# A second seven-product group in the output projection of the last layer

## The chip, the core and the metric

The kernel runs on one core of a Trainium2 chip. Its time is the device time of one execution in microseconds, as the median of several runs; less is better. Before the change it takes 1976.4 us (median of 3 runs, 1975.78 to 1977.06). Engines are named as the profile names them: PE (TensorE, matmuls), PEld (its weight loads), DVE (VectorE), ACT (ScalarE), POOL (GpSimd, which here only issues DMAs), SP (SyncE, which issues most DMAs).

## What is computed

Two layers of a decoder trunk over 256 tokens of width 2048, in float32. Each layer normalises its input, makes one wide projection, runs three token mixers on it (A: sparse attention, B: a convolution module, C: stick-breaking attention), projects each mixer's output to the model width, merges the three with sigmoid gates, and adds an output projection to the residual:

```python
y_a = (dsa_attention(qa, ka, va, qi, ki, wi, top_k) * jax.nn.silu(za)) @ w_a_out
y_b = (conformer_conv(ub, conv_w, conv_b, cln_w, cln_b) * jax.nn.silu(zb)) @ w_b_out
y_c = (stick_breaking_attention(qc, kc, vc) * jax.nn.silu(zc)) @ w_c_out
g = jax.nn.sigmoid(gates).reshape(b, s, N_BRANCH, D_MODEL)
merged = g[:, :, 0] * y_a + g[:, :, 1] * y_b + g[:, :, 2] * y_c
return x + merged @ w_out
```

After the second layer a last RMSNorm closes the trunk. The change touches `merged @ w_out` of the second layer: 256 tokens x 2048 (K) times 2048 x 2048.

## The kernel before

**Split numbers.** Each float32 operand is split in a high part (a cast, on ACT) and a low part (the rest, on DVE), and a product is three matmuls: high x high, low x high, high x low. Weights come from DRAM in units of 256 rows (K) x 512 columns, 512 KB, into a `raw` buffer (five, and `va` as a sixth). `high` casts a unit into `wh` (L296), `low` writes `raw - wh` into `wl` (L300). There are three pairs of `wh` and `wl`, so a unit's pair comes free when PE has done the unit three places before it; both run two steps ahead of PE.

**Steps.** `run` goes through a list of steps that is written out by hand with `gather`. A *plain* unit is twelve matmuls (3 products x 2 token tiles x 2 rows of 128). A *half step* is six and belongs to a `Seven`.

**Seven products.** `Seven` does a block product of 2 token tiles x 2 halves of a K range x 2 column blocks with seven block products instead of eight (M1 to M7, each in halves a and b). Four of them (M5, M6, M7, M4) take sums of weight blocks, and three (M5 to M7, M3) sums of token blocks. The weight sums are made in *homes*: buffers into which two blocks are loaded (`two`, `three`), added on DVE (L555, L570, or L557, L558 in another form) and on the way in by accumulating DMAs that POOL issues (L545, L576). A number `adds` chooses the form: 3 uses three DVE sums per half and one accumulating DMA, 4 uses two and two. The results build up in four PSUM banks X, Y, Z, W; banks are copied (L621, ACT) and subtracted (L627, DVE) on the way. A step's `at` hangs work on it, such as these sums.

**The stage.** The last layer ends so: a group `h1` for gates of branch B, with the first eight units of B's output product (`y1`) among its steps; the other eight y units (columns 1024 to 1535, then 1536 to 2047); and the output projection. Each four y units complete one of four column blocks j of the merged activations. That block is multiplied and added (L1612, L1613), transposed on DVE (L340), sent through DRAM in DMAs from POOL (`z`, L343, and back as `zy`, L349), and split again by ACT and DVE (L713, L714) into `mx`, the left operand of the output projection. The number LATER says how many steps after its product a block is split. `output_sums` makes the token sums from blocks j = 0 and 1.

**The output projection before.** One group `o` does columns 0 to 1023 for the first half of K (rows 0 to 1023). Everything else is plain units: c (columns 1024 to 1535, eight units), d (1536 to 2047, first half of K, four units), e and f (0 to 511 and 512 to 1023, second half of K, four units each). Units of the second half of K need j = 2 (their first two) and j = 3. Each finished column block is added to the residual (`emit_x`, L1646 or L1649). Columns 1536 to 2047, second half, come last: their four weight units are loaded and split (L285, into `s`), and 54 matmuls follow behind the last step, then the norm and the output.

`o`'s homes before are the buffers `ar`, `ph` and `pl`, which the groups before it also use. `slot()` gives one of 13 buffers of 8 KB a partition (`s8`).

Of the kernel before, what the change touches and what calls it, by code (L numbers as in the profile page):

```python
# [89 lines left out]
def trunk(ctx: ExitStack, tc: tile.TileContext, x, w_in, xt, w_a, w_b, w_c, w_out,  # L90
# [54 lines left out]
    def slot(dt=F32):  # L145
        return sp.tile([P, KC, S], dt, tag="s8", bufs=13, name=nm("s8"))
# [668 lines left out]
    for layer in range(DEPTH):  # L815
# [775 lines left out]
        def mg(j, t, mgs=mgs):  # L1591
            return mgs[j // 2][:, j % 2, t, :]
# [85 lines left out]
        def merged(b, j, y):  # L1678
            sg = held.pop((b, j), None)
            with in_turn() if b == 1 else nullcontext():  # L1680
                merge(b, j, y, sg)
            if b == 1:
                with in_turn():
                    turned([mg(j, t) for t in range(NT)], partial(use_m, j), LATER - 3 * (j in (1, 3) and not last), soon=True)

        kept_x, acc3 = {}, once(wide_accs)

        def output(q, banks, k0):
            if last and q == 3:
# [66 lines left out]

        zg["M4", 1].at(1, partial(gate_summed, 0))
        zg["M3", 1].at(1, partial(gate_summed, 1))
        for i, st in enumerate((y1[2][3], f1[0]) if not last else y1[3][:2]):
            st.at(0, partial(output_sums, i * 2, i * 2 + 1))  # L1760
        if last:
            zd[3].at(0, lambda: nc.sync.dma_start(fwl[0], fnw.partition_broadcast(P)))
        if last:
            o = Seven(wo, (p0 * 512, p0 * 512 + 512), mx, osums, 10, None, 3)
            qs = {}
            for q in range(4):
                own = q in (p0, p0 + 1)
                banks = (lambda v: lambda: [o.bank(n) for n in v])("ZW" if q - p0 else "XY") if own else None
                qs[q] = output(q, banks, KC if own else 0)
# [21 lines left out]
        steps += gather(thin + rest, y=y2[10:], g=g1, c=c1, d=d1)  # L1791
        if last:
            steps += gather("y*2 " + begin.replace("M6a y", "M6a").replace("M2a y", "M2a") + rest, g=h1, y=y1[:8], c=e1, d=f1)
            steps += y1[8:]
        else:
            steps += gather("y*2 " + begin.replace("M6a y", "M6a").replace("M2a y", "M2a") +
                            "g.M3a c g.M3b c g.M4a c g.M4b c y*4", g=h1, y=y1[:12], c=e1)
# [10 lines left out]
        steps[at_norm].at(0, norm)  # L1808
        c, d = 2 - p0, 3 - p0
        if last:  # L1810
            steps += qs[c][:4] + gather(
                "g.M1a d g.M5a g.M1b d g.M5b d g.M6a d g.M6b c g.M2a c g.M2b g.M7a g.M7b g.M3a e g.M3b e g.M4a f g.M4b f c*2 e*2 f*2",
                g=o, c=qs[c][4:], d=qs[d], e=qs[p0], f=qs[p0 + 1])
        else:
            second = ("n.M1a h n.M1b h*3 y n.M5a y n.M5b y n.M6a n.M6b y n.M2a n.M2b n.M7a n.M7b "
                       "o.M1a c o.M1b d o.M5a c o.M5b d o.M6a n.M4a o.M6b n.M4b c*2 o.M2a d o.M2b o.M7a o.M7b n.M3a n.M3b d "
                       "o.M3a e o.M3b e o.M4a e o.M4b e f*4")
            steps += gather(second, n=n, o=o, y=y1[12:], h=f1, c=qs[c], d=qs[d], e=qs[p0], f=qs[p0 + 1])
# [15 lines left out]
            nc.vector.tensor_scalar(half, known, -0.5 / D, -0.5 * EPS, op0=ALU.mult, op1=ALU.add)  # L1834
            nc.vector.tensor_scalar(known, known, 1.0 / D, EPS, op0=ALU.mult, op1=ALU.add)

        c0, n = 1536, 512
        xc = residual(c0, n)

        head = acc3()  # L1840
        accs = [head[0], acc_tile()]
        nc.vector.tensor_add(xc[:, 1, :], head[1], xc[:, 1, :])
        oh, ol = ([slot(F32R).rearrange("p (k a) t -> p k (a t)", a=2) for _ in range(2)] for _ in range(2))
        for k0 in range(0, KC, 2):
            ks = slice(k0 % 4, k0 % 4 + 2)
            unit(w_out[layer], KC + k0, 2, [(c0, n)], dst=(oh[k0 // 4][:, ks, :], ol[k0 // 4][:, ks, :]))
        for t in range(NT):
            m, r, b = (small(1) for _ in range(3))
            kn, hf, ss = known[:, t:t + 1], half[:, t:t + 1], ssq[:, t, 3:4]
            if t < NT - 1:  # L1850
                for h in range(2):
                    token_products([accs[t]], n, (oh[h], ol[h]), mx, KC + h * 4, 4, KD, [t])
                emit_x(xc, [accs[t]], 3, c0, [t])
            else:

                token_products([accs[t]], n, (oh[0], ol[0]), mx, KC, 4, KD, [t], KC)
                token_products([accs[t]], n, (oh[1], ol[1]), mx, KC + 4, 2, KD - 2, [t], KC)
# [85 lines left out]
```

## Time and profile before

| | us |
|---|---|
| median of 3 runs | 1976.4 |
| the profiled execution | 1976.76 |
| its span, first to last instruction | 1974.7 |
| PE busy | 1962.6 |
| DVE busy | 1724.7 |
| ACT busy | 1357.5 |
| POOL busy | 234.2 |
| first y unit behind h1 starts | 1859.64 |
| last step of the output projection ends | 1954.86 |

The time lies 2.1 us over the span; the rest is before the first and behind the last instruction. Busy times overlap, since the engines work side by side. In a row of the timeline the first number is the start in us from the span's start, the second its duration; "x8" are instructions in a row, and in square brackets stands how long the engine had idled and what ended that. A row of a window has, after its length, the busy times of PE, PEld, DVE, ACT and POOL (with counts), the granted clock of TensorE, the mean busy share of the DMA engines and their GB/s. Names of tiles stand without their numbers: `wl<-raw,wh` is any split of a weight unit.

### The profile page before, as it was taken

Reading aid. Unit: us, or ns where it says so; the run is one execution under the profiler, and the core shown is the slowest. Engines: PE = TensorE matmul, PEld = TensorE weight load, DVE = VectorE, ACT = ScalarE, POOL = GpSimd, SP = SyncE. Lnnn points to the kernel's source line nnn. Section 1 sums busy time; section 2 is a strip of 40 time slices with the busy share of each in tenths; the row PEclk is TensorE's granted clock in tenths of the full one; section 3 lists DMA queues with packets and bytes.
Section 4 is the critical chain, followed back from the end, with each engine's and each line's share of the span. In section 5 each row is a group of like instructions: output and inputs, shape, how many; then the busy total and the mean of one; then the engine's idle time right before and its main releaser. Section 6 shows DMA issues by size and latency. Waiting matters only on the chain.

```text
span 1974.7 us, 26272 instructions
## 1 busy us (share of the span) xinstructions
PE 1962.6 (99%) x9158; PEld 1642.7 (83%) x9158; DVE 1724.7 (87%) x2022; ACT 1357.5 (69%) x1782; POOL 234.2 (12%) x354
## 2 busy tenths in 40 slices
PE   9999999999999999999999999999999999999998
PEld 8888888888888888887888888888888888888886
DVE  8788999988998899889896988999889988898786
ACT  7567657679887666565665666676798876765654
POOL 0011102210100001012200211112101000011010
PEclk9999999999999999999999999999999999999999
DMA  7778759765888779889967787688659787798883
GB/s 276 279 253 270 238 188 315 266 226 190 257 265 268 235 243 297 268 288 322 331 232 277 250 270 233 199 294 280 218 180 290 246 285 249 242 294 270 288 279 136
DMA packets 147205, 507.86 MB, mean 257 GB/s; under 512 B 18368, under 2 KB 22976, under 8 KB 146944
## 3 DMA queue, kind: packets, MB, share of 16 engines
q1 hardware_dynamic: 116832, 409.18, 58.4%
q0 software_dynamic: 28576, 93.87, 19.0%
q10 hardware_dynamic: 1664, 3.15, 0.4%
q8 instruction: 71, 1.16, 0.2%
q14 instruction: 62, 0.51, 0.1%
HBM read 473.35 MB, written 32.77 MB: 256 GB/s over the span
## 4 chain that ended last, share of the span: by engine, by line
PE 98%; DVE 1%; issue 0%; DMA 0%; ACT 0%; DVEq 0%
PE acc L311 67%; PE mm L311 28%; PE mm L1313 1%; PE mm L1404 0%; PE mm L1455 0%; PE mm L1508 0%; PE mm L1371 0%; DVE wl L300 0%; PE mm L1485 0%; DMA raw<-in_w_in_dram 0%; PE mm L1284 0%; PE mm L1374 0%; PE mm L1513 0%; PE mm L1458 0%; DVE zt L340 0%
## 5 line engine op out<-in xcount | busy, mean ns | idle before, releaser
L311 PE MATMUL acc<-wh,s 128*128 128x512 f32 x3952 | 1007.8, 391 | 2.2 <-DVE s L714 1.1
L296 ACT CAST wh<-raw 128x1024 fp32r<-128x1024 f32 x636 | 663.4, 1046 | 376.7 <-PE acc L311 234.4
L300 DVE TENSOR_TENSOR wl<-raw,wh 128x1024 fp32r<-128x1024 f32 (+1 forms) x637 | 767.8, 1211 | 159.2 <-ACT wh L296 157.1
L311 PEld LDWEIGHTS acc<-wh,s 128*128 128x128 f32 x3952 | 734.7, 188 | 151.3 <-DVE acc L627 2.1
L311 PE MATMUL acc<-wl,s 128*128 128x512 f32 x1784 | 498.8, 390 | 0.1
L311 PEld LDWEIGHTS acc<-wl,s 128*128 128x128 f32 x1784 | 333.9, 188 | 71.2 <-DVE wl L300 2.0
L311 PE MATMUL mm<-wh,s 128*128 128x512 f32 (+1 forms) x1496 | 365.8, 385 | 0.0
L311 PEld LDWEIGHTS mm<-wh,s 128*128 128x128 f32 x1496 | 279.7, 188 | 54.6
L311 PE MATMUL mm<-wl,s 128*128 128x512 f32 (+1 forms) x748 | 198.2, 385 | 0.0
L343 POOL DMA_DIRECT2D z<-zt x192 | 113.8, 608 | 692.8 <-DVE zt L340 656.9
L311 PEld LDWEIGHTS mm<-wl,s 128*128 128x128 f32 x748 | 139.9, 188 | 27.0 <-DVE wl L300 0.4
L296 ACT CAST wh<-ar 128x1024 fp32r<-128x1024 f32 x92 | 96.9, 1053 | 71.7 <-PE acc L311 36.3
L300 DVE TENSOR_TENSOR wl<-ar,wh 128x1024 fp32r<-128x1024 f32 x92 | 111.7, 1219 | 15.2 <-ACT wh L296 14.3
L300 DVE TENSOR_TENSOR wl<-va,wh 128x1024 fp32r<-128x1024 f32 x52 | 63.5, 1220 | 18.0 <-ACT wh L296 17.7
L296 ACT CAST wh<-va 128x1024 fp32r<-128x1024 f32 x52 | 54.4, 1046 | 32.6 <-PE acc L311 13.7
L349 POOL DMA_DIRECT2D zy<-z x50 | 36.4, 729 | 300.0 <-DMA z<-zt 85.2
L311 PEld LDWEIGHTS mm<-s,wl 128*128 128x128 f32 x512 | 66.9, 191 | 5.0
L779 DVE SCALAR_TENSOR_TENSOR s<-yT,cst,s 128x256 f32<-128x256 f32 x160 | 69.2, 475 | 0.0
L311 PE MATMUL mm<-s,wl 128*128 128x192 f32 x512 | 66.0, 271 | 0.0
L774 ACT ACTIVATE zt<-yT,cst 128x256 f32<-128x256 f32 x128 | 57.5, 502 | 8.2 <-DVE s L1083 8.0
L774 ACT ACTIVATE ar<-yT,cst 128x256 f32<-128x256 f32 x136 | 60.3, 502 | 2.9 <-PE mm L1374 2.3
L774 ACT ACTIVATE s<-yT,cst 128x256 f32<-128x256 f32 x72 | 33.3, 521 | 30.2 <-DVE s L1083 30.1
(303 smaller groups left out, 1587.6 us busy)
## 6 DMA issues: line engine op xcount, KB each, us to landing
raw<-in_w_in_dram SPq DMA_DIRECT2D x497, 512.0 KB, 4.5
raw<-in_w_out_dram SPq DMA_DIRECT2D x49, 512.0 KB, 5.5
zy<-z POOLq DMA_DIRECT2D x48, 512.0 KB, 5.7
z<-zt POOLq DMA_DIRECT2D x184, 128.0 KB, 5.1
ar<-in_w_in_dram SPq DMA_DIRECT2D x28, 512.0 KB, 6.2
ar<-in_w_in_dram POOLq DMA_DIRECT2D x28, 512.0 KB, 8.4
raw<-in_w_a_dram SPq DMA_DIRECT2D x26, 512.0 KB, 6.5
raw<-in_w_b_dram SPq DMA_DIRECT2D x25, 512.0 KB, 4.2
```

The costliest lines, as they stand in the source:

```text
L296: newest_parts[0] = nc.scalar.copy(u[1], u[0])
L300: newest_parts[1] = sub = nc.vector.tensor_sub(u[2], u[0], u[1].bitcast(F32))
L311: newest[0] = nc.tensor.matmul(o, lhsT, rhs, start=start, stop=stop, skip_group_check=True)
L343: nc.gpsimd.dma_start(z[:, :, :, a, :].rearrange("t b c e -> c (t b) e"), tmp[a * 32:(a + 1) * 32].rearrange("c t b k i -> c (t b) (k i)"))
L349: nc.gpsimd.dma_start(y.rearrange("p (t a) k i -> p t (a k i)", a=4), z.rearrange("t b c a e -> (b c) t (a e)"))
L774: nc.scalar.activation(v, yT[:, c, q:q + S], AF.Identity if bias else AF.Copy, scale=wq, **b)
L779: nc.vector.scalar_tensor_tensor(o, yT[:, c, q:q + S], wq, o, op0=ALU.mult, op1=ALU.add)
L1313: nc.tensor.matmul(ps[:, q * S:(q + 1) * S], qi[i][:, hd, :], ki[j][:, 0, :], start=n == 0, stop=n == 2)
```

## The change

In the last layer a second group `n` takes columns 1024 to 2047 for the first half of K. The plain units c and d of that half go; c keeps its four units of the second half. The homes of `o` move to two slots of their own (`places`), and `n` has `ar`, `ph` and `pl`. Both use form 4. `n`'s banks are the two wide tiles that the y products used, so the tile `acc3` for columns 1536 to 2047 goes too: its sums now stand in n's banks Z and W. The eight y units, which stood ahead of `o`, now stand between `o`'s half steps, and so the token sums are made earlier (at the second and third of h1's d units, f1, instead of at y units), and each merged block is split three steps sooner.

```diff
-                    turned([mg(j, t) for t in range(NT)], partial(use_m, j), LATER - 3 * (j in (1, 3) and not last), soon=True)
+                    turned([mg(j, t) for t in range(NT)], partial(use_m, j), LATER - 3 * (last or j in (1, 3)), soon=True)
...
             if last and q == 3:
-                return [plain(wo, k, q * 512, mx, acc3, k == 0, False) for k in range(0, KC, 2)]
+                return []
...
-        for i, st in enumerate((y1[2][3], f1[0]) if not last else y1[3][:2]):
+        for i, st in enumerate((y1[2][3], f1[0]) if not last else (f1[1], f1[2])):
             st.at(0, partial(output_sums, i * 2, i * 2 + 1))
...
-            o = Seven(wo, (p0 * 512, p0 * 512 + 512), mx, osums, 10, None, 3)
...
+            places = [once(lambda: slot().rearrange("p a b -> p (a b)")) for _ in range(2)]
+            o = Seven(wo, (0, 512), mx, osums, 10, None, 4, places)
+            n = Seven(wo, (1024, 1536), mx, osums, 10, None, 4, None, True)
+            qs = {q: output(q, lambda g=g, v=v: [g.bank(i) for i in v], KC)
+                  for q, g, v in ((0, o, "XY"), (1, o, "ZW"), (2, n, "XY"), (3, n, "ZW"))}
...
-            steps += y1[8:]
...
-            steps += qs[c][:4] + gather(
-                "g.M1a d g.M5a g.M1b d g.M5b d g.M6a d g.M6b c g.M2a c g.M2b g.M7a g.M7b g.M3a e g.M3b e g.M4a f g.M4b f c*2 e*2 f*2",
+            steps += gather("o.M1a y o.M1b y o.M5a y o.M5b y o.M6a y o.M6b y o.M2a y o.M2b y o.M7a o.M7b "
+                            "o.M3a o.M3b e*2 o.M4a f o.M4b f n.M1a n.M1b n.M5a e n.M5b e n.M6a f n.M6b f "
+                            "n.M2a n.M2b n.M7a n.M7b n.M3a c n.M3b c n.M4a c n.M4b c",
...
-        head = acc3()
+        head = [n.bank("Z"), n.bank("W")]
```

The order of DVE where block j = 2 of `mx` gets its low half, before. The L714 is that of j = 2; `wl_3111` and `wl_3117` are the splits of o.M6a and o.M6b (from `ar`), and the others those of plain units.

```order
L300 TENSOR_TENSOR wl_3102_16655<-ar_81,wh_3101_16654 128x1024
L300 TENSOR_TENSOR wl_3106_16670<-raw_3087_16590,wh_3105_16669 128x1024
L570 TENSOR_TENSOR ar_81<-pl_3059_16423,raw_3076_16525 128x1024
L300 TENSOR_TENSOR wl_3111_16693<-ar_81,wh_3110_16692 128x1024
L300 TENSOR_TENSOR wl_3115_16707<-raw_3093_16619,wh_3114_16706 128x1024
L714 TENSOR_TENSOR s8_3107_16685<-zy_3073_16507,s8_3107_16685 128x4x256
L300 TENSOR_TENSOR wl_3117_16723<-ar_81,wh_3116_16722 128x1024
```

And now. The rows are, in this order: the split of o.M3a, the product of the last y block (j = 3) with its gate, the split of o.M3b, the sum, bank W, the two transposes of j = 3, the splits of the first and second e unit and of o.M4a, and then L714 of j = 2.

```order
L300 TENSOR_TENSOR wl_3102_16631<-raw_3084_16545,wh_3101_16630 128x1024
L1612 TENSOR_TENSOR t4_3049_16377<-mm_3080_16520,t4_3049_16377 128x1024
L300 TENSOR_TENSOR wl_3107_16653<-raw_3088_16565,wh_3106_16652 128x1024
L1613 TENSOR_TENSOR s8_2559_13922<-s8_2559_13922,t4_3049_16377 128x1024
L627 TENSOR_TENSOR acc_3062_16435<-ev_3069_16474,acc_3056_16409 128x512
L340 STREAM_TRANSPOSE zt_3103_16642<-s8_2559_13922 128x4x4x32 x2
L300 TENSOR_TENSOR wl_3110_16667<-raw_3091_16578,wh_3109_16666 128x1024
L300 TENSOR_TENSOR wl_3113_16679<-va_3094_16596,wh_3112_16678 128x1024
L300 TENSOR_TENSOR wl_3117_16694<-s8_3019_16207,wh_3116_16693 128x1024
L714 TENSOR_TENSOR s8_3114_16688<-zy_3087_16563,s8_3114_16688 128x4x256
```

The low half of j = 2 stood between o.M6a and o.M6b and now stands behind the whole work on j = 3, and behind the splits of both e units that multiply it. On ACT the cast of j = 2 (L713) stands behind the cast of the second e unit and ahead of that of o.M4a.

The order of ACT at the end, before: the casts of the last units, then those of the four units of columns 1536 to 2047 (`s8`), with the squares of a finished block between.

```order
L296 CAST wh_3171_17004<-raw_3156_16920 128x1024
L1654 ACTIVATE ev_3173_17021,sm_2371_12903<-t4_3159_16938 128x512
L296 CAST wh_3176_17028<-va_3160_16940 128x1024
L1654 ACTIVATE ev_3173_17021,sm_2371_12903<-t4_3159_16938 128x512
L296 CAST s8_3184_17091<-raw_3188_17095 128x1024
L296 CAST s8_3184_17091<-raw_3189_17099 128x1024
L296 CAST s8_3185_17092<-raw_3190_17103 128x1024
L296 CAST s8_3185_17092<-raw_3191_17107 128x1024
```

And now, where `wh_3181`, `wh_3183`, `wh_3185`, `wh_3188` and `wh_3190` are the casts of the second c unit, n.M4a, the third c unit, n.M4b and the last c unit:

```order
L296 CAST wh_3181_17015<-raw_3167_16949 128x1024
L296 CAST s8_3197_17119<-raw_3201_17123 128x1024
L296 CAST wh_3183_17031<-ar_81 128x1024
L296 CAST s8_3197_17119<-raw_3202_17127 128x1024
L296 CAST wh_3185_17041<-raw_3173_16980 128x1024
L296 CAST s8_3198_17120<-raw_3203_17131 128x1024
L296 CAST wh_3188_17059<-ar_81 128x1024
L296 CAST s8_3198_17120<-raw_3204_17135 128x1024
L296 CAST wh_3190_17069<-raw_3178_17003 128x1024
```

The four casts into `s8` now stand between those of the last steps, each ahead of one that PE needs. The load of `raw_3201` waits for the split of n.M3a, whose buffer it takes, and that of `raw_3204` for the split of `raw_3201`.

More of the change, by code (lines that the diff above doesn't have):

```diff
@@ L1683, in merged @@
                 with in_turn():
-                    turned([mg(j, t) for t in range(NT)], partial(use_m, j), LATER - 3 * (j in (1, 3) and not last), soon=True)
-        kept_x, acc3 = {}, once(wide_accs)
+                    turned([mg(j, t) for t in range(NT)], partial(use_m, j), LATER - 3 * (last or j in (1, 3)), soon=True)
+        kept_x = {}
         def output(q, banks, k0):
             if last and q == 3:
-                return [plain(wo, k, q * 512, mx, acc3, k == 0, False) for k in range(0, KC, 2)]
+                return []
             def finished():
@@ L1763, in trunk @@
         if last:
-            o = Seven(wo, (p0 * 512, p0 * 512 + 512), mx, osums, 10, None, 3)
[L1765 to L1769, printed above, removed]
+            places = [once(lambda: slot().rearrange("p a b -> p (a b)")) for _ in range(2)]
[3 more added lines that the diff above has]
+                  for q, g, v in ((0, o, "XY"), (1, o, "ZW"), (2, n, "XY"), (3, n, "ZW"))}
         else:
@@ L1810, in trunk @@
         if last:
-            steps += qs[c][:4] + gather(
-                "g.M1a d g.M5a g.M1b d g.M5b d g.M6a d g.M6b c g.M2a c g.M2b g.M7a g.M7b g.M3a e g.M3b e g.M4a f g.M4b f c*2 e*2 f*2",
-                g=o, c=qs[c][4:], d=qs[d], e=qs[p0], f=qs[p0 + 1])
+            steps += gather("o.M1a y o.M1b y o.M5a y o.M5b y o.M6a y o.M6b y o.M2a y o.M2b y o.M7a o.M7b "
+                            "o.M3a o.M3b e*2 o.M4a f o.M4b f n.M1a n.M1b n.M5a e n.M5b e n.M6a f n.M6b f "
+                            "n.M2a n.M2b n.M7a n.M7b n.M3a c n.M3b c n.M4a c n.M4b c",
+                            n=n, o=o, y=y1[8:], c=qs[2], e=qs[0], f=qs[1])
         else:
@@ L1835, in trunk @@
             nc.vector.tensor_scalar(known, known, 1.0 / D, EPS, op0=ALU.mult, op1=ALU.add)
-        c0, n = 1536, 512
-        xc = residual(c0, n)
-        head = acc3()
+        c0, width = 1536, 512
+        xc = residual(c0, width)
+        head = [n.bank("Z"), n.bank("W")]
         accs = [head[0], acc_tile()]
@@ L1845, in trunk @@
             ks = slice(k0 % 4, k0 % 4 + 2)
-            unit(w_out[layer], KC + k0, 2, [(c0, n)], dst=(oh[k0 // 4][:, ks, :], ol[k0 // 4][:, ks, :]))
+            unit(w_out[layer], KC + k0, 2, [(c0, width)], dst=(oh[k0 // 4][:, ks, :], ol[k0 // 4][:, ks, :]))
         for t in range(NT):
@@ L1851, in trunk @@
                 for h in range(2):
-                    token_products([accs[t]], n, (oh[h], ol[h]), mx, KC + h * 4, 4, KD, [t])
+                    token_products([accs[t]], width, (oh[h], ol[h]), mx, KC + h * 4, 4, KD, [t])
                 emit_x(xc, [accs[t]], 3, c0, [t])
             else:
-                token_products([accs[t]], n, (oh[0], ol[0]), mx, KC, 4, KD, [t], KC)
-                token_products([accs[t]], n, (oh[1], ol[1]), mx, KC + 4, 2, KD - 2, [t], KC)
+                token_products([accs[t]], width, (oh[0], ol[0]), mx, KC, 4, KD, [t], KC)
+                token_products([accs[t]], width, (oh[1], ol[1]), mx, KC + 4, 2, KD - 2, [t], KC)
                 with tc.high_priority(offset=URGENT):
```

## The prediction

> **What bounds the kernel now.** I read the page first (busy shares and the chain of waits), then the timeline of each engine over the last 115 us, then the windows of the stage that the change rewrites.
>
> ```profile
> PE 1962.6 (99%) x9158; PEld 1642.7 (83%) x9158; DVE 1724.7 (87%) x2022; ACT 1357.5 (69%) x1782; POOL 234.2 (12%) x354
> PE 98%; DVE 1%; issue 0%; DMA 0%; ACT 0%; DVEq 0%
> L311 PE MATMUL acc<-wh,s 128*128 128x512 f32 x3952 | 1007.8, 391 | 2.2 <-DVE s L714 1.1
> L296 ACT CAST wh<-raw 128x1024 fp32r<-128x1024 f32 x636 | 663.4, 1046 | 376.7 <-PE acc L311 234.4
> 1859.64:1892.00 32.36, 32.36 (x144) 26.82 (x143) 29.30 (x35) 17.17 (x21) 5.39 (x9) 1.00 0.93 336
> 1892.00:1955.00 63.00, 63.00 (x279) 52.08 (x279) 50.56 (x48) 38.18 (x44) 2.56 (x3) 1.00 0.62 202
> ```
>
> The second row is the chain that ended last: 98% of the span is TensorE (PE). The third, its largest group, waited 2.2 us in the whole kernel, the fourth prices a cast at 1.05 us. The last two are windows, with busy times in the order PE, PEld, DVE, ACT, POOL. They hold the stage in question, from the first y unit after the h1 group (1859.64) to the last unit of the output projection (1954.86). PE has no gap in it, so a matmul taken away shortens the stage by its own time, as long as nothing takes PE's place. The second engine is VectorE (DVE): 29.30 + 50.56 = 79.86 of 95.36 us, 84%.
>
> ```profile
> 1859.64 1.98 PE L311 MATMUL mm<-wh,s 128*128 128x512 f32 x8
> 1862.37 1.98 PE L311 MATMUL mm<-wh,s 128*128 128x512 f32 x8
> 1881.40 1.98 PE L311 MATMUL mm<-wh,s 128*128 128x512 f32 x8
> 1919.50 1.07 PE L311 MATMUL acc<-wh,s 128*128 128x512 f32 x4
> 1920.86 1.07 PE L311 MATMUL acc<-wh,s 128*128 128x512 f32 x4
> 1954.86 5.60 PE L311 MATMUL mm<-s,s 128*128 128x512 f32 x24
> ```
>
> Matmuls overlap in their records, so I take distances between starts. A plain unit of twelve takes 1862.37 - 1859.64 = 2.72 us, a half step of six 1920.86 - 1919.50 = 1.36 us: 0.227 us a matmul.
>
> **The change part by part.**
>
> *Matmuls.* For columns 1024 to 2047 and the first half of K, eight plain units (96 matmuls) become fourteen half steps (84). Twelve fewer at 0.227 us: **-2.72 us**. The rest of the stage has the same units in another order, and the 54 matmuls behind 1954.86 and the chain behind them stay.
>
> *Work added on the other engines.* Six more casts and six more splits (L296, L300), since each half step needs both as a plain unit does; weight sums four per group, so eight for two groups instead of six; two more subtractions L627 and two copies L621; eight more transfers of 512 KB, two on SP and six on POOL. The prices on DVE:
>
> ```profile
> 1854.59 1.22 DVE L300 TENSOR_TENSOR wl<-raw,wh 128x1024 fp32r<-128x1024 f32 x1 [1.50 <-ACT wh L296]
> 1881.79 1.22 DVE L300 TENSOR_TENSOR wl<-raw,wh 128x1024 fp32r<-128x1024 f32 x1 [1.50 <-ACT wh L296]
> 1882.93 1.22 DVE L1612 TENSOR_TENSOR t<-mm,t 128x1024 f32<-128x1024 f32 x1
> 1886.46 1.30 DVE L340 STREAM_TRANSPOSE zt<-s 128x512 f32<-128x512 f32 x2
> 1887.68 1.18 DVE L557 TENSOR_TENSOR ph<-ph,ar 128x1024 f32<-128x1024 f32 x1
> 1905.20 1.22 DVE L714 TENSOR_TENSOR s<-zy,s 128x1024 fp32r<-128x1024 f32 x1
> 1922.83 0.69 DVE L627 TENSOR_TENSOR acc<-ev,acc 128x512 f32<-128x512 f32 x1
> 1923.43 1.22 DVE L300 TENSOR_TENSOR wl<-raw,wh 128x1024 fp32r<-128x1024 f32 x1
> 1924.57 1.22 DVE L714 TENSOR_TENSOR s<-zy,s 128x1024 fp32r<-128x1024 f32 x1
> 1925.70 1.22 DVE L300 TENSOR_TENSOR wl<-raw,wh 128x1024 fp32r<-128x1024 f32 x1
> ```
>
> From start to start a 1024-wide operation costs 1.14 us, a 512-wide one 0.60, a pair of transposes 1.22. So DVE gains 8 x 1.14 + 2 x 0.60 = 10.3 us: 90 of the 92.6 us that PE would need. All of it lies beside PE on average, but DVE works in its order and has hardly any room left to catch up. What matters is therefore where its order puts an operation that PE waits for.
>
> *The place where PE is late: the first e unit.* It multiplies columns 1024 to 1535 of the merged activations (j = 2), whose low half L714 writes. Let T0 be the end of the fourth y unit (the one behind o.M5b, which completes j = 2) and T1 the end of the eighth. Between them lie four half steps and four units: T1 = T0 + 16.3. PE reaches the first e unit four half steps after T1, at T1 + 5.44, does its four high products, and needs the low half at T1 + 5.44 + 0.91 = **T1 + 6.35**.
>
> DVE, by the order shown above, does ten things between T1 and the end of that L714. The first, the split of o.M3a, goes into the buffer of the eighth y unit, and comes 1881.79 - 1881.40 = 0.39 us behind its end, as it does before. Then: split M3a, product L1612, split M3b, sum L1613 (4 x 1.14), L627 (0.60), transposes (1.22), splits of e, e and o.M4a (3 x 1.14), L714 (1.22): 0.39 + 4.56 + 0.60 + 1.22 + 3.42 + 1.22 = **T1 + 11.4**. None of these waits for the e units, and the chain can't start before T1. The stall is 11.4 - 6.35 = **+5.06 us**. Before, the same L714 (at 1905.20) stood far ahead of its user, behind plain units that gave DVE 2.72 us each. The trace has such a stall once, in layer 0, where PE did two high products and then waited for L714:
>
> ```profile
> 897.45 1.28 DVE L714 TENSOR_TENSOR s<-s,s 128x512 fp32r<-128x512 f32 x2
> 898.18 0.73 PE L311 MATMUL acc<-wh,s 128*128 128x512 f32 x2 [1.06 <-DVE s L714]
> ```
>
> *The same place from the side of the DMA.* The cast L713 of j = 2 waits for the way through DRAM, and the cast of o.M4a stands behind it on ACT, which DVE needs at T1 + 9.05 = T0 + 25.4. With 1.04 us for L713 and 1.05 for the cast, the data must land by T0 + 23.3.
>
> ```profile
> 1813.43 1.22 DVE L1612 TENSOR_TENSOR t<-mm,t 128x1024 f32<-128x1024 f32 x1
> 1816.22 0.86 POOL L576 DMA_DIRECT2D ar<-in_w_in_dram  x1 [1.55 <-DVE wl L300]
> 1819.56 2.40 POOL L343 DMA_DIRECT2D z<-zt  x4 [2.48 <-DVE zt L340]
> 1829.59 0.71 POOL L349 DMA_DIRECT2D zy<-z  x1 [7.63 <-DMA z<-zt]
> 1877.22 2.33 POOL L343 DMA_DIRECT2D z<-zt  x4 [31.53 <-DVE zt L340]
> 1885.39 0.72 POOL L349 DMA_DIRECT2D zy<-z  x1 [5.85 <-DMA z<-zt]
> zy<-z POOLq DMA_DIRECT2D x1, 512.0 KB, 6.4
> zy<-z POOLq DMA_DIRECT2D x1, 512.0 KB, 9.2
> zy<-z POOLq DMA_DIRECT2D x1, 512.0 KB, 4.9
> 1900.31 1.04 ACT L713 CAST s<-zy 128x1024 fp32r<-128x1024 f32 x1
> ```
>
> L1612 starts 1.53 us behind its unit (1882.93 - 1881.40). In the h1 group, with two accumulating transfers L576 just ahead as there will be here, z follows L1612 by 6.13 us and zy follows z by 10.0; without them by 8.2. So zy goes out at T0 + 15.8 to 17.7 and lands 4.9 to 9.2 us later. With 6.4 that is T0 + 22.2 to 24.1, just around the limit: 0 to 0.8 us more, I take **+0.2**. With 9.2 it is 1.7 to 3.6 us more.
>
> *The rest, costed at nothing.* The second activation (j = 3) goes to the third e unit, 23 us of PE behind T1, and DVE reaches its L714 with the stall's 5 us in hand. The token sums move ahead, to d units, where DVE idled 1.50 us a unit (the row at 1854.59); their cover is small (about 0.3 us at the half steps M1b and M5a) and they would cost about 1 us if zy of j = 1 landed 2 us later. o's homes land in slots that the h1 group has left, some 20 us before their use. At the end, ACT takes the casts of the last four weight units between those of the last steps. From the split of n.M3a two loads follow one another there: 4.2 (load), 1.05 (cast), 1.14 (split), 4.2, and two casts, 12.7 us, against 13.6 us that PE needs from n.M3a to the last c unit. Nothing, then, with loads of 4.2 us, and 2 us more for each us that a load takes longer.
>
> ```profile
> raw<-in_w_out_dram SPq DMA_DIRECT2D x4, 512.0 KB, 4.2
> raw<-in_w_out_dram SPq DMA_DIRECT2D x4, 512.0 KB, 6.4
> ```
>
> *Sum:* -2.72 + 5.06 + 0.2 = **+2.5 us**: span 1974.7 to 1977.2. The profiled execution took 1976.76, 2.1 beyond its span, and lies 0.4 over the median of the runs, so 1976.4 + 2.5 = **1978.9 us**.
>
> **The rivals.** 0.2% (4 us) is about what a measurement of this kernel can tell from no change; less than that counts as the same.
>
> *The saving stands.* If DVE keeps ahead at the e unit, because splits come sooner than I lay them, 1976.4 - 2.7 = 1973.7, still within 0.2%. For it: PE's largest group waited only 2.2 us in 1974.7 before. Against it: the ten operations are fixed behind T1 by their inputs, their buffers or their place in DVE's order. Chance 0.13.
>
> *Transfers land late (slower).* Eight more transfers, six of them accumulating ones on the queue that carries z and zy, in a stage where the DMA share is already 0.93. It decides from a landing of zy of about 8 us, or of the last raw loads of 6.4: then 1.7 to 3.6 us at the e unit and up to 2 x 2.2 - 0.9 = 3.5 at the end. At the middle of the first and half of the second it is 1978.7 + 2.6 + 1.8 = 1983.1 (1978.7 being the forecast without its 0.2); with one of the two alone about 1981. Against it: at the end the DMA share is low. Chance 0.18.
>
> *The clock falls in the wait (slower).*
>
> ```profile
> 1966.00:1975.00 9.00, 0.00 (x0) 0.00 (x0) 3.82 (x14) 1.93 (x6) 0.00 (x0) 0.67 0.57 218
> ```
>
> In the 9 us behind the last matmul the granted clock (the third last number) averages 0.67, not 1.00. If a stall of 5 us brings 5 us at 0.67 behind it, that is 5 x (1/0.67 - 1) = 2.5 us more: 1981.4. Against it: the wait is cut in two by the four high products, and the shorter waits of layer 0 left no mark. Chance 0.13. [...] The row agrees that the clock falls in idling; no row before shows the price of a fall in mid-kernel.
>
> *Faster by more than 4 us* would need more than the twelve matmuls. 0.04 for what I don't see.
>
> **How the numbers follow.** Forecast 0.52 (1978.9), saving stands 0.13, late transfers 0.18, clock 0.13, more 0.04. Same: 0.52 + 0.13 = 0.65. Slower: 0.18 + 0.13 = 0.31. Faster: 0.04. The forecast's own range is 1977 to 1980.3. For eight in ten I leave out the lowest tenth (most of "saving stands") and the dearest late transfers: 1974.6 to 1982.4.
>
> **What would show it.** Right: PE waits between 4 and 6 us in one piece of the stage, released by L714 at the first e unit, four to twelve matmuls into the columns 0 to 511 group; the twelve matmuls are gone; all else in the stage without gaps; the last unit's end 2 to 3 us later than 1954.86. Wrong: PE runs through the e units (then the DVE layout is false), or the larger wait stands at the last c unit behind ACT's casts, at n.M7 behind accumulating transfers, or ahead of T0 at o.M1b or o.M5a behind the token sums. A granted clock under 1.00 behind the wait would show the third rival.

## The result and the profile after

The change makes the kernel slower: 1987.8 us (median of 6 runs, 1986.1 to 1989.0) against 1976.6 (6 runs, 1975.3 to 1978.0), a ratio of 1.0056 with a 95% interval of 1.0043 to 1.0069. The forecast was 1978.9, with a range up to 1982.4. The profiled execution of the change spans 1984.6 us, 9.9 more than before. It took 1986.4 us, 1.4 under the median, so a little over 1 us of the 11.2 between the medians is in no trace.

The busy times of the page first (the columns are busy time, share of the span, number of instructions), then PE's largest group of instructions; both after the change:

```profile
PE 1964.9 (99%) x9146; PEld 1641.3 (83%) x9146; DVE 1734.8 (87%) x2033; ACT 1364.1 (69%) x1790; POOL 239.5 (12%) x360
L311 PE MATMUL acc<-wh,s 128*128 128x512 f32 x3952 | 1010.9, 391 | 7.5 <-ACT s L713 2.8
```

PE has its twelve matmuls less (9146 for 9158) and yet more busy time (1964.9 for 1962.6): some matmuls ran slower (four took 2.07 us at 1904.19, and 1.07 at 1861.02). And the largest group now waits 7.5 us in place of 2.2. The timeline of PE in the stage, after the change, shows where (start, duration, instruction, and in brackets the idle time ahead of it):

```profile
1848.33 1.98 PE L311 MATMUL acc<-wh,s 128*128 128x512 f32 x8
1853.77 1.98 PE L311 MATMUL acc<-wh,s 128*128 128x512 f32 x8
1858.13 2.14 PE L311 MATMUL acc<-wh,s 128*128 128x512 f32 x8 [1.48 <-ACT wh L296]
1861.02 1.07 PE L311 MATMUL acc<-wh,s 128*128 128x512 f32 x4
1866.99 0.74 PE L311 MATMUL acc<-wl,s 128*128 128x512 f32 x2 [0.72 <-DVE wl L300]
1867.58 2.02 PE L311 MATMUL mm<-wh,s 128*128 128x512 f32 x8
1871.67 0.73 PE L311 MATMUL acc<-wh,s 128*128 128x512 f32 x2 [0.71 <-DVE s L714]
1872.70 1.99 PE L311 MATMUL mm<-wh,s 128*128 128x512 f32 x8
1904.19 2.07 PE L311 MATMUL acc<-wh,s 128*128 128x512 f32 x4 [2.75 <-ACT s L713]
1907.53 2.07 PE L311 MATMUL acc<-wh,s 128*128 128x512 f32 x4 [1.27 <-DVE s L714]
1911.08 2.02 PE L311 MATMUL acc<-wh,s 128*128 128x512 f32 x8
1948.32 1.16 PE L311 MATMUL mm<-wh,s 128*128 128x512 f32 x4 [1.48 <-DVE mm L627]
1964.74 5.60 PE L311 MATMUL mm<-s,s 128*128 128x512 f32 x24
```

From start to start, against 2.72 us a plain unit and 1.36 a half step, these rows give what each place lost:

| place | steps between the rows | nominal | took | lost |
|---|---|---|---|---|
| last d unit of h1, 1853.77 to 1861.02 | 2 plain | 5.44 | 7.25 | 1.81 |
| o.M1b, to 1867.58 | 1 plain, 2 half | 5.44 | 6.56 | 1.12 |
| o.M5a, to 1872.70 | 1 plain, 1 half | 4.08 | 5.12 | 1.04 |
| ahead of the first e unit, to 1904.19 | 6 plain, 9 half | 28.56 | 31.49 | 2.93 |
| in the first e unit, to 1911.08 | 1 plain | 2.72 | 6.89 | 4.17 |
| n.M3a, to 1948.32 | 7 plain, 12 half | 35.36 | 37.24 | 1.88 |
| the rest, to 1964.74 | 4 plain, 4 half | 16.32 | 16.42 | 0.10 |

The sum is 13.05 us. With the twelve matmuls that went, 2.72 us, the stretch from the last c unit of h1 (1848.33) to the 24 matmuls behind the last step (1964.74) should be 10.3 us longer. It took 116.4 us; before, from 1848.77 (the row below) to 1954.86, it took 106.1: 10.3 longer. So there are three losses, 4.0 us around h1's end and o's start, 7.1 us at the first e unit, and 1.9 us at n.M3a. The forecast had the second, at 5.3.

```profile
1848.77 1.98 PE L311 MATMUL acc<-wh,s 128*128 128x512 f32 x8
```

This stretch is the measure in what follows, since the runs of one kernel spread over 3 to 7 us. Without any wait it would take 106.1 - 2.7 = 103.4 us.

The first loss, on ACT and POOL (timelines and transfers; the first two rows are from before, the rest from after the change):

```profile
1844.97 0.72 POOL L349 DMA_DIRECT2D zy<-z  x1 [4.58 <-DVE wl L300]
zy<-z POOLq DMA_DIRECT2D x1, 512.0 KB, 6.8
1846.45 0.72 POOL L349 DMA_DIRECT2D zy<-z  x1 [6.33 <-ACT wh L296]
1855.13 1.05 ACT L713 CAST s<-zy 128x1024 fp32r<-128x1024 f32 x1 [6.46 <-DMA zy<-z]
1857.03 1.04 ACT L296 CAST wh<-raw 128x1024 fp32r<-128x1024 f32 x1
zy<-z POOLq DMA_DIRECT2D x1, 512.0 KB, 8.7
```

The transfer zy brings block j = 1 back. It took 8.7 us to land (the last row), and 6.8 before. It also went out later: 8.7 us behind the block's first z (1837.79), and 6.9 before (z at 1838.06). So the block was back 3.6 us later behind its z than before. ACT took its operations in the order of the program. L713 of block 1 stands three units sooner in that order than before, and the cast of h1's last d unit stands behind it: ACT idled 6.46 us, and the cast came at 1857.03. The token sums follow from the same L713, and o.M1b and o.M5a wait behind them on DVE.

The second loss, on ACT and DVE and in windows (busy times of PE, PEld, DVE, ACT, POOL, then the granted clock, the DMA share and GB/s), after the change:

```profile
1903.09 1.04 ACT L713 CAST s<-zy 128x1024 fp32r<-128x1024 f32 x1 [2.38 <-DMA zy<-z]
1905.11 1.23 DVE L300 TENSOR_TENSOR wl<-s,wh 128x1024 fp32r<-128x1024 f32 x1 [0.22 <-ACT wh L296]
1906.26 1.22 DVE L714 TENSOR_TENSOR s<-zy,s 128x1024 fp32r<-128x1024 f32 x1
1901.00:1904.20 3.20, 0.45 (x3) 0.03 (x2) 3.20 (x5) 1.11 (x2) 1.25 (x3) 1.00 1.02 401
1904.20:1907.50 3.30, 2.06 (x4) 1.15 (x4) 3.06 (x3) 0.88 (x1) 1.09 (x2) 0.50 1.03 408
1907.50:1911.10 3.60, 3.57 (x9) 2.82 (x10) 0.00 (x0) 1.04 (x1) 0.00 (x0) 0.51 1.03 404
```

L713 of block 2 starts when its transfer has landed. DVE is busy all through the wait (3.20 of 3.20 us), waits 0.22 us for the cast behind L713, and reaches L714 of block 2 at 1906.26. When the matmuls are let go, the granted clock is 0.50, for 6.8 us (1904.2 to 1911.0).

The third loss on DVE, and behind it the same place of group o (the subtraction on DVE, o.M3b on PE), all after the change:

```profile
1946.35 1.22 DVE L300 TENSOR_TENSOR wl<-va,wh 128x1024 fp32r<-128x1024 f32 x1
1947.48 0.69 DVE L627 TENSOR_TENSOR mm<-ev,mm 128x512 f32<-128x512 f32 x1
1900.76 0.69 DVE L627 TENSOR_TENSOR acc<-ev,acc 128x512 f32<-128x512 f32 x1
1899.91 1.07 PE L311 MATMUL acc<-wh,s 128*128 128x512 f32 x4
```

L627 computes bank W from bank Y behind n.M7b. n.M3a adds into bank Z and needs neither. But n's banks are wide tiles of two, X with Y and Z with W, and n.M3a starts 0.15 us behind the end of L627. In o, which has a tile for each bank, o.M3b starts 0.85 us ahead of the same subtraction. From this contrast I take it that the wait stands on the tile; no run gives n a tile for each bank.

### The profile page after: what moved, and what is told of

Same layout as the page of the kernel before. It is cut to its first block, busy times and chain, and to the rows that moved or that the text cites. A ratio compares the mean times of both kernels' runs of the same rounds, so it can differ in the third digit from the quotient of the medians.

```text
span 1984.6 us, 26299 instructions
## 1 busy us (share of the span) xinstructions
PE 1964.9 (99%) x9146; PEld 1641.3 (83%) x9146; DVE 1734.8 (87%) x2033; ACT 1364.1 (69%) x1790; POOL 239.5 (12%) x360
```

## The experiments

They are numbered e1 to e11. In all of them "the change" is the kernel above. Stretches are from the last c unit of h1 to the 24 matmuls, from one trace each, that of one run. That run lies within 1.0 us of its kernel's median, but for the change (1.4 under it) and e8 (2.6 under it).

**e1. Another block at the first e units.** Is the data of block 2 what comes late there?

```diff
-            steps = [plain(wo, k, q * 512, mx, banks, k == 0, k == KD - 2) for k in range(k0, KD, 2)]
+            steps = [plain(wo, k, q * 512, {2: mx[0]} if last and q == 0 and k < KC + 4 else mx, banks, k == 0, k == KD - 2)
+                     for k in range(k0, KD, 2)]
```

> The change, but the first two e units multiply block 0 of the merged activations, which has long been split, where they should multiply block j = 2; the same number of matmuls, loads, casts and splits. (Part of the result is another one for that.) In the trace of the change the first e unit starts 2.91 us late (2.75 of them waiting for L713), waits 1.27 us more for L714 and takes 6.89 us in all in place of 2.72: 7.08 us lost there. Theory A, the split of j = 2 is what comes late: all of it goes, the first e unit takes 2.72 us, and the time falls by 7.1 us from 1987.8 to 1980.7. Rival B, the e units are late through their own weights (load, cast or split behind an overloaded DVE or DMA): a wait of 3 us or more stays there, and the time falls by less than 3. Rival C, the wait only moves to the first f unit, the next that multiplies j = 2: by the trace the L714 ends 1.5 us before that unit would need it, so under A no wait over 0.3 us is there; under C 2 us or more.

1982.35 us (9 runs), ratio to before 1.0028, interval 1.0018 to 1.0038: 5.4 less than the change. The stretch took 111.2, 5.2 less. The two longer of PE's waits from 1900 to 1925 in its timeline:

```profile
1904.37 1.19 PE L311 MATMUL acc<-wl,s 128*128 128x512 f32 x4 [0.56 <-DVE wl L300]
1921.19 1.19 PE L311 MATMUL acc<-wh,s 128*128 128x512 f32 x4 [0.66 <-ACT s L713]
```

The 4.0 us of waiting for block 2 and the slow clock are gone, so theory A holds: it was the data. Two smaller waits that had been hidden behind it came up. The split of the first e unit's own weights is late by 0.56 us (DVE is that far behind), and the third e unit, the first user of block 3, now waits for its L713. The places lose 0.85 and 1.52 us: 7.1 - 0.85 - 1.52 = 4.7, and 0.3 less were lost at h1's end. Of rivals B and C there is that much, 2.4 us, though at other places than C had it: the f unit did not wait.

**e2. TensorE kept busy in the wait.** Is the slow stretch a consequence of idling?

```diff
+            def fill(w_, count):
+                for _ in range(count):
+                    mult(n.bank("X"), part(mx, 0, 0, 1, slice(0, P))[:, 0, :], w_[0][:, 0, :], True, False)
+
+            def filled(w_):
+                fill(w_, 12)
+                for i, j in ((0, 0), (1, 0), (0, 1)):
+                    if i:
+                        fill(w_, 10)
...
+            e_first.mm = filled
```

> The change, with 22 matmuls whose results nobody uses: 12 ahead of the first e unit and 10 between its four high products and its low ones, into a bank that the group n overwrites later. At 0.227 us each they fill 2.7 and 2.3 us of the wait for L713 and L714 and wait only for data that is there. Theory A, the slow stretch at the e unit (twelve matmuls from 1904.19 on at a granted clock of 0.53 to 0.62) comes from TensorE's having idled: with the idle time filled the clock stays at 1.00, the e unit's low products take 1.8 us in place of 3.55, and the time falls by 1.7 us to 1986.1, though TensorE does 5 us more work. Rival B, the slow stretch has another cause (DVE or the weights hold the matmuls back): the time stays at 1987.8 or grows by up to what the 22 matmuls delay, and the granted clock stays under 0.7 there.

1987.68 us (5 runs, 1985.2 to 1989.1), ratio 1.0051 [1.0039, 1.0064]: in the times no difference from the change can be seen. In the trace it can. PE's timeline at the first e unit, and a window:

```profile
1903.96 2.88 PE L311 MATMUL mm<-wh,s 128*128 128x512 f32 x12
1907.07 1.20 PE L311 MATMUL acc<-wh,s 128*128 128x512 f32 x4 [0.24 <-ACT s L713]
1908.11 2.45 PE L311 MATMUL mm<-wh,s 128*128 128x512 f32 x10
1912.39 1.99 PE L311 MATMUL acc<-wh,s 128*128 128x512 f32 x8
1907.00:1910.00 3.00, 2.93 (x13) 2.41 (x14) 2.58 (x3) 0.97 (x2) 0.98 (x2) 1.00 1.04 412
```

The first and third rows are the fillers, the fourth is the second e unit. The clock stays at 1.00, where it fell in all four traces in which the e unit waited unfilled (the change, e3, e4, e5). From where the e unit could start without a wait to its end (1903.96 to 1912.39) it takes 8.4 us, where in the change it took 9.8 (2.93 + 6.89), with 5 us of matmuls more in it. The stretch is 114.9, 1.5 shorter: theory A's 1.7, within what the fillers overshoot. So the first e unit's 7.1 us are 5.3 of late data and 1.7 of slow clock. That the run times don't show it stays so; five runs with a spread of 4 us could not.

**e3. The loads of o's homes later.** Why was block 1 late?

```diff
-            o = Seven(wo, (0, 512), mx, osums, 10, None, 4, places)
+            o = Seven(wo, (0, 512), mx, osums, 7, None, 4, places)
```

> The change, with the loads of o's homes asked for three steps later (lead 7 in place of 10). In the trace of the change the transfer that brings block j = 1 back (zy) takes 8.7 us to land among these loads, ACT stands 6.46 us in front of L713 until 1855.1, and the unit behind, then o.M1b and o.M5a, lose 1.8 + 1.0 + 1.0 us. Theory A, the landing is late because the loads of the homes share the DMA engines with it: it lands in about 6.8 us as before the change, L713 starts by 1853.3, the wait at the d unit goes and those at o.M1b and o.M5a shrink or go: 1.9 to 3.6 us less, 1984.2 to 1985.9. Rival B, only the place of L713 (three units sooner in ACT's order) counts and the transfer takes as long without the loads: unchanged, 1987.8.

1983.66 us (5 runs), ratio 1.0039 [1.0026, 1.0051]: 4.1 less than the change. From its timelines:

```profile
1850.07 1.05 ACT L713 CAST s<-zy 128x1024 fp32r<-128x1024 f32 x1 [1.93 <-DMA zy<-z]
1900.04 2.08 PE L311 MATMUL acc<-wh,s 128*128 128x512 f32 x4 [3.12 <-ACT s L713]
1904.00:1908.00 4.00, 4.00 (x11) 3.13 (x10) 0.75 (x1) 1.04 (x1) 0.72 (x1) 0.50 1.03 408
```

ACT waits 1.93 us in front of L713 of block 1 in place of 6.46, and all three waits at h1's end and o's start are gone: theory A, 4.0 us. The stretch is only 2.5 shorter (113.9), since the first e unit lost 8.6 us this time: the clock was at 0.50 from 1899.0 to 1909.1, 10.1 us in place of 6.8 (more on that below).

**e4. Block 1 split a unit later.** The place or the landing?

```diff
-   ... LATER - 3 * (last or j in (1, 3)), soon=True)
+   ... (7,8,7,7)[j] if last else LATER - 3 * (j in (1, 3)), soon=True)
-        for i, st in enumerate((y1[2][3], f1[0]) if not last else (f1[1], f1[2])):
+        for i, st in enumerate((y1[2][3], f1[0]) if not last else (f1[2], f1[3])):
```

> The change, with block j = 1 split one unit later (and the token sums that need it one step later). Theory A, what counts is when block 1 lands (1855.1): the wait at the d unit (1.5 us) goes, since its cast is no longer behind L713, but the chain L713, L714, sums, o.M5a starts from the same landing, so the waits at o.M1b and o.M5a grow by about as much: 1987.8 within 1 us. Rival B, the place of L713 in ACT's order makes the loss: all three waits go, 1984.2. The waits at the first e unit and at n.M3a stay under both.

1986.21 us (5 runs, 1984.1 to 1989.5), ratio 1.0045 [1.0032, 1.0057]. The stretch took 115.2, 1.2 less. The wait at the d unit is gone, and the others remain; the first e unit lost 0.6 us more than in the change:

```profile
1865.81 0.73 PE L311 MATMUL acc<-wl,s 128*128 128x512 f32 x2 [0.43 <-DVE wl L300]
1870.89 0.73 PE L311 MATMUL acc<-wh,s 128*128 128x512 f32 x2 [1.14 <-DVE s L714]
```

At h1's end and o's start 2.2 us are lost where the change lost 4.0. Neither theory has it quite right: 1.8 us came from the place of L713 ahead of the cast, 2.2 from the landing. With a landing in time (the run before) both go.

**e5. An f unit between n.M7b and n.M3a.**

```diff
-  n.M5a e n.M5b e n.M6a f n.M6b f n.M2a n.M2b n.M7a n.M7b n.M3a c ...
+  n.M5a e n.M5b n.M6a e n.M6b f n.M2a n.M2b n.M7a n.M7b f n.M3a c ...
```

> The change, with one e unit and one f unit a place later, so that an f unit stands between n.M7b and n.M3a (where nothing stood) and none between n.M5b and n.M6a. In the trace of the change n.M3a starts 1.9 us late, 1.48 of them put down to L627, which subtracts into bank W and reads bank Y; n's banks come in wide tiles of two (X with Y, Z with W), so n.M3a, which adds into Z, waits for the whole tile. In group o, with a tile for each bank, the same subtraction ended after o.M3b had begun, and nothing waited. Theory A, the wait is this shared tile: with 2.7 us of an f unit between, it goes, and nothing takes its place: the stretch from the last c unit of h1 to the last 54 matmuls takes 114.5 in place of 116.4 us, the time 1.9 us less (1985.9, little more than the spread of the runs, so the trace decides). Rival B, DVE is simply late there with its splits: a wait of over 1 us appears at n.M6a or n.M3a, and the stretch stays at 116 us or more.

1985.84 us (5 runs), ratio 1.0045 [1.0032, 1.0059]. n.M3a doesn't wait, and no wait appears elsewhere behind the e unit, as theory A says. That rules out rival B; an f unit in between would cover any wait for that subtraction, though, and so doesn't test the tile by itself. The stretch is 115.4, 1.0 shorter and not 1.9, because the first e unit, which this edit doesn't touch, was slower again by about the difference:

```profile
1908.04 2.07 PE L311 MATMUL acc<-wh,s 128*128 128x512 f32 x4 [2.15 <-DVE s L714]
1911.61 2.98 PE L311 MATMUL acc<-wh,s 128*128 128x512 f32 x8
```

The eight matmuls of the second e unit took 2.98 us here, 2.02 in the change: the slow clock (0.50) began later (near 1907) and reached into that unit.

**e6. Block 2 done earlier.** The four y units of block 2 go ahead of the last three units of h1; o keeps the four of block 3.

```diff
-  (h1)  ... g.M4b c c d*3
+  (h1)  ... g.M4b c c y*4 d*3
-  o.M1a y o.M1b y o.M5a y o.M5b y o.M6a y o.M6b y o.M2a y o.M2b y o.M7a o.M7b o.M3a o.M3b e*2 ...
+  o.M1a o.M1b y o.M5a o.M5b y o.M6a o.M6b y o.M2a o.M2b y o.M7a o.M7b o.M3a o.M3b e*2 ...
```

> The change, with the y units of block j = 2 (four) ahead of the last three units of h1, and only the four of block j = 3 between o's half steps. Block 2 is then done 8 us sooner by the steps of PE, its split has left DVE before o.M7, and o.M5a comes three half steps later behind the landing of block 1. Theory A, the waits at h1's last unit, o.M1b and o.M5a (4.0 us together) and the one at the first e unit with its slow clock (7.1 us) are one and the same thing, merged blocks asked for too soon behind their products: both go, 1987.8 - 11.1 = 1976.7; n.M3a's 1.9 us stay; the stretch from the last c unit of h1 takes about 105.3 us. Rival B, DVE cannot keep up between o's half steps, now that only every second pair has a plain unit beside it (two splits and one sum are 3.4 us for 2.7 us of two half steps): waits for L300 of 2 us or more between o.M5a and o.M7b, 1979 or more.

1981.56 us (11 runs), ratio 1.0023 [1.0014, 1.0032]: 6.2 less than the change, not 11.1. The stretch took 110.9, 5.5 less. The waits of theory A are gone but for 0.56 us behind the split of the first e unit's weights, and n.M3a's stayed. A new one stands at o.M2b (PE and ACT):

```profile
1890.34 1.21 PE L311 MATMUL acc<-wh,s 128*128 128x512 f32 x4 [2.36 <-ACT wh L296]
1888.30 1.04 ACT L713 CAST s<-zy 128x1024 fp32r<-128x1024 f32 x1 [5.12 <-DMA zy<-z]
```

It is not rival B, which had DVE late. It is the first loss over again, with block 2 in place of block 1: L713 waits for its transfer, o.M2b's cast stands behind it, and the clock falls behind the wait (0.50 from 1892.0 to 1895.3); 4.8 us went there.

**e7. Both remedies**, and **e8. the loads later as well**:

```diff
-  ... o.M3a o.M3b e*2 o.M4a f o.M4b f n.M1a n.M1b n.M5a e n.M5b e n.M6a f n.M6b f n.M2a n.M2b n.M7a n.M7b n.M3a c ...
+  ... o.M3a e o.M3b e o.M4a f o.M4b n.M1a n.M1b n.M5a f n.M5b e n.M6a e n.M6b f n.M2a n.M2b n.M7a n.M7b f n.M3a c ...
```

> The order of e6_head, with an f unit between n.M7b and n.M3a, and the e and f units spread one by one over the half steps from o.M3a on. Theory A, with all four waits gone the twelve matmuls saved show in the time: 1976.8 - 2.7 = 1974.1, up to 1 us more if a small wait of DVE is left; the stretch from the last c unit of h1 takes 103.4 to 104.4 us against 106.1 before the change. Rival B, the group costs more than it saves wherever it stands, since DVE has 90 us of work for 92.6: waits of 2 us or more appear elsewhere, and the time is 1976.8 or more.

> The order of e7_head_fill, with the loads of o's homes asked for three steps later. If the loads still hold up the way of block 1 through DRAM in the new order, this one is faster than e7_head_fill by the wait that is left at h1's last units (up to 1.8 us); if, with more steps between, nothing waits for block 1, the two are the same within 0.5 us in the trace.

e7: 1979.95 us (11 runs), ratio 1.0014 [1.0005, 1.0023], stretch 110.9. e8, with the lead of 7 for o: 1979.45 (11 runs), ratio 1.0013 [1.0004, 1.0022], stretch 106.5. Theory A of e7 fails at the same place, where 5.7 us went:

```profile
1891.75 1.20 PE L311 MATMUL acc<-wh,s 128*128 128x512 f32 x4 [3.27 <-ACT wh L296]
```

So rival B's numbers came true, for the most part with another cause than DVE: a wait of 1.21 us for the split of o.M1b (at 1872.76), which e6 and e8 don't have, cost 1.4 us more. n.M3a doesn't wait any more. In e8 the wait at o.M2b is 1.42 us, and the clock stays at 1.00. The times of the two can't be told apart. Their traces differ by 4.4 us, but the run traced for e8 took the least time of its eleven, 2.6 us under the median, so what the later loads are worth in this order stays open.

**e9. The splits later again**, and **e10. n's loads later**:

```diff
-   ... LATER - 3 * (last or j in (1, 3)), soon=True)
+   ... (8,8,10,8)[j] if last else LATER - 3 * (j in (1, 3)), soon=True)     (e9; e10: 8, 8, 9, 8)
-            n = Seven(wo, (1024, 1536), mx, osums, 10, None, 4, None, True)
+            n = Seven(wo, (1024, 1536), mx, osums, 8, None, 4, None, True)   (e10 alone)
```

> The order of e8_head_fill_lead7, with the splits of the four blocks later again: 8, 8, 10 and 8 units behind their products in place of 7 (block 2, with no user before the first e unit, gets all three back). In e8 the stretch from the last c unit of h1 took 106.5 us, 3.1 more than the 103.4 that the matmuls alone need: ACT stood 4.18 us in front of L713 of block 2 (its zy took 8.6 us to land, with a DMA share of 1.05), a weight cast of o stood behind it, and PE waited 1.42 and 0.25 us there and 0.43 us later at an e unit. Theory A, an early place of L713 in ACT's order turns a late landing into a wait of the weight casts: with L713 of block 2 eight us later nothing stands behind it in vain; the stretch takes 103.4 to 104.4 us, the time is 2 to 2.7 us under before. Rival B, the DMA engines are full and what waits is the weights themselves: the wait changes its name to a cast or split behind a raw load and stays above 2 us in sum, the stretch at 105.5 or more.

> As e9_late_again, with block 2 split 9 units behind its product and the loads of n's homes asked for two steps later (lead 8 in place of 10), so that they keep off the way of block 2 through DRAM. Theory A of e9: the same as e9 within 0.7 us. If the share of the DMA engines still sets a wait in e9 (rival B), this one has less of it, and n.M5 or n.M7 may wait for its homes instead (L570, or L300 from ar, ph or pl).

e9: 1977.96 us (11 runs), ratio 1.0007 [0.9998, 1.0016], stretch 106.9. e10: 1977.30 (11 runs), ratio 0.9999 [0.9990, 1.0007], stretch 106.7. Nothing waits behind L713 of block 2 now, but 3.5 and 3.3 us are still lost: rival B. (The stretch is no shorter than that of e8, whose traced run lay far under its median; by the medians e9 is 1.5 us faster than e8, and the intervals of the two overlap.) The wait had moved to the next thing that comes through the DMA engines. ACT, the transfers between 1870 and 1900, and a window, in e10:

```profile
1891.67 1.05 ACT L296 CAST wh<-s 128x1024 fp32r<-128x1024 f32 x1 [1.77 <-DMA s<-in_w_out_dram]
s<-in_w_out_dram POOLq DMA_DIRECT2D x4, 512.0 KB, 13.6
1880.00:1900.00 20.00, 19.18 (x84) 15.25 (x83) 16.05 (x16) 11.27 (x11) 2.14 (x3) 1.00 1.04 299
```

The cast is that of o.M7b, from its home; the four transfers are o's accumulating ones, all sent within 5 us. They took 13.6 us to land.

**e11. Two of the four accumulating transfers earlier.** Form 2 has as many sums and transfers as form 4, but sends L545 with the loads of the homes.

```diff
-            o = Seven(wo, (0, 512), mx, osums, 7, None, 4, places)
+            o = Seven(wo, (0, 512), mx, osums, 7, None, 2, places)
```

> The order of e10_late_lead, with group o in form 2 in place of 4 (n stays at 4): the same number of sums on DVE and of accumulating transfers, but two of o's four (L545) go out with the loads of the homes, some 20 us ahead of o.M5, and not behind the second sum. In e10 all four went out between 1877.1 and 1882.2 and took 13.6 us to land (median), while the DMA engines were full (share 1.04) and moved 270 to 300 GB/s in place of 400; the cast of o.M7b stood 1.77 us in front of its home, DVE got behind, and PE lost 0.76 us at o.M4a; the stretch from the last c unit of h1 took 106.65 us, 3.3 over what its matmuls need. Theory A, the bunch of accumulating transfers is what is left: with two of them gone from there the cast of o.M7b waits under 0.3 us, the stretch falls to 105.5 us or less (1976.1 or less). Rival B, the DMA engines are short of time over the whole stage and whatever moves only moves the wait: the stretch stays at 106.2 or more, with a wait on ACT for L713 or a raw load in another place.

1973.89 us (11 runs, 1973.1 to 1976.8) against 1977.28 of the kernel before on the same chip (15 runs): ratio 0.9985, interval 0.9976 to 0.9994. This is faster than the kernel before, by 3.4 us in the medians and 1.2 to 4.7 by the interval, and than the change. POOL, a window and PE's timeline:

```profile
1858.55 0.95 POOL L545 DMA_DIRECT2D s<-in_w_out_dram  x1 [12.24 <-DMA s<-in_w_out_dram]
1862.25 0.89 POOL L545 DMA_DIRECT2D s<-in_w_out_dram  x1 [2.76 <-DMA s<-in_w_out_dram]
1880.00:1900.00 20.00, 20.00 (x90) 16.35 (x89) 17.33 (x18) 12.21 (x14) 1.95 (x3) 1.00 0.98 324
1919.94 1.20 PE L311 MATMUL acc<-wh,s 128*128 128x512 f32 x4 [0.35 <-DVE s L714]
1953.39 5.60 PE L311 MATMUL mm<-s,s 128*128 128x512 f32 x24
```

The two L545 went out 17 to 19 us sooner than in e10 (1877.06 and 1879.43). The cast of o.M7b doesn't wait, as theory A says. PE is busy for all of 1880 to 1900, and a single wait of 0.35 us is left in the stage. The stretch, from 1849.24, is 104.15 us: 1.9 under before, 0.8 over what the matmuls alone need. The expectation for this run put e10's longest wait of PE (0.76 us, on L627) at o.M4a; by the program it is the first e unit's, in bank Y, which L627 has to read first.

## Why the prediction was wrong

**The matmuls, -2.72: right in size.** The last run has the same twelve matmuls less, and a stretch 1.9 us shorter than before with 0.8 us of losses left: 2.7 us.

**The first e unit, +5.06: right in place, cause and size.** T1, the end of the eighth y unit, is 1893.12 + 2.72 = 1895.84. L714 was to end at T1 + 11.4 and ended at 1907.48, T1 + 11.6. The low products were to start at T1 + 6.35 = 1902.2 and did at 1907.53: 5.3 us. The transfer of block 2 was laid at T0 + 22.2 to 24.1; T0 is 1876.80 + 2.72 = 1879.52, and L713 started right on it at 1903.09, T0 + 23.6. The 0.2 us that this was to cost are the 0.22 that DVE waited for the cast behind L713. The two causes ended almost together, and no run parts them. With DVE free, L714 could have followed L713 and ended near 1905.4, so the landing alone would have cost about 3.2 us (an estimate from these rows), where the order of DVE alone was laid at 5.06.

**The clock: put among the rivals, and it belonged in the sum.** The prediction gave the fall of the clock a chance of 0.13, against it that the four high products cut the wait in two. They did not help, since they waited too: their block's high half came 2.75 us late, so that one idle stretch came ahead of them. The forecast had not held its own two numbers side by side: a landing at T0 + 22.2 to 24.1, with 1.04 us of L713 behind it, against an e unit that starts at T1 + 5.44 = T0 + 21.7. Its price was 1.7 us. The clock was at 0.50 for 6.8 us. The first half of that fell into the wait for L714, where slow matmuls cost nothing: the four high products took 2.07 us in place of 1.07, and PE still waited 1.27 us behind them. In the second half the low products took 3.55 us (1907.53 to 1911.08) in place of 8 x 0.227 = 1.81. The rival's 2.5 from the 0.67 of the kernel's end was too high here. In e3 and e5 the price was 2.8, half of the 5.7 us from the start of the low products (1903.38 and 1908.04) to the end of the slow clock.

**"The rest, costed at nothing": wrong by 5.9 us, and the step that failed.** Two losses were in it.

The first is h1's end, 4.0 us. The prediction had weighed the token sums alone, and laid "about 1 us if zy of j = 1 landed 2 us later". It landed 3.6 us later behind its z than before, of which 1.9 are zy's own (8.7 in place of 6.8). The same edit moved L713 of block 1 ahead of the casts of h1's last units, and what is queued behind it on ACT was not asked for block 1, only for block 2. And the homes of o were looked at for when they are used ("some 20 us before their use"), not for whose way they cross: their four loads went out beside block 1's way through DRAM, and with those later (e3) the 4.0 us were gone.

The second is n.M3a, 1.9 us. The prediction watched n.M7's accumulating transfers, which were in time. It did not ask what waits for L627 in n. o has a tile for each bank and n has one for two, and the subtraction that nothing waited for in o held up the next product in n; with a unit in between the wait was gone (e5).

**The tail chain, at nothing: right.** The last row of the table lost 0.10 us.

**The range.** Its upper end, 1982.4, came from weighing the clock and the late transfers as alternatives to the forecast. They were additions to it: 5.3 + 1.7 + 4.0 + 1.9 - 2.7 = 10.2. Late transfers, the rival with 0.18, were right as a mechanism, but neither of its two places (block 2 and the last raw loads) was where it struck.

## What to carry to other kernels

An operation that waits for a transfer, moved forward on an engine that works in order, makes everything behind it wait for that transfer (ACT idled 6.46 us in front of L713 of block 1, and 5.12 us in front of that of block 2 in e6, each time with the cast of a weight unit behind it): ask of each such move what stands behind it, block by block, and add the losses up, since they don't exclude each other. New loads are judged by what they run beside as much as by when they are needed; sending two accumulating transfers some 18 us earlier was worth 2.5 us in the traces (e10, e11). A saving on the engine that bounds is only had when all its feeders have kept their lead: with the same twelve matmuls less, the kernel was 11.2 us slower in one order and 3.4 us faster in another (1.9 by the stretch).

## What the hardware showed

The slow clock lasted about 3.4 us, or two or three times that. By windows of 1 us the granted clock was 0.50 from 1904.2 to 1911.0 in the change (6.8 us), from 1899.0 to 1909.1 in e3 (10.1), from 1904.6 to 1911.4 in e4 (6.8), from 1907.0 to 1913.7 in e5 (6.7), from 1892.0 to 1895.3 in e6 (3.4) and from 1893.5 to 1896.9 in e7 (3.4). In e6 and e7 it fell 1.6 and 1.8 us after PE had set to work again, and in e6 PE had waited only 2.36 us. In e5 it fell in PE's second wait. The waits of 1.42 us (e8) and 1.48 us (n.M3a in the change) left no mark: the clock stayed at 1.00. Three windows of e6, with the clock as the third last number:

```profile
1891.00:1892.00 1.00, 0.77 (x4) 0.33 (x3) 1.00 (x2) 1.00 (x2) 0.00 (x0) 0.97 1.05 279
1892.00:1893.00 1.00, 1.00 (x3) 0.82 (x3) 1.00 (x2) 1.00 (x2) 0.00 (x0) 0.50 1.02 274
1895.00:1896.00 1.00, 1.00 (x5) 0.78 (x4) 0.14 (x1) 0.03 (x1) 0.00 (x0) 0.83 1.02 270
```

So the slow clock at the first e unit cost 1.7 us (the change) or up to 2.8 (e3, e5) on top of the waits, by where it fell. What sets these lengths, and what decides when the clock falls, no run shows.

While accumulating transfers were under way, the DMA engines moved less: with four of them (e10, 1880 to 1900) they were full (share 1.04) at 299 GB/s, where in the change, with none under way, they were as full (1.02) at 401 (the windows above). The change itself shows the same: 261 and 274 GB/s at a share of 1.06 in the windows 1880 to 1885 and 1885 to 1890, in which its own were landing.
